# Two weight sums of a seven-product scheme moved into adding transfers, with six row tiles per block in place of five

## The chip, the cores and the metric

The kernel runs on one core of one Trainium2 chip. The metric is the device time of one execution in microseconds (us): the median of three runs, which lie between 1940.07 and 1940.61 us. One further execution was recorded by the profiler; its rows are what the text reads.

## The reference

One encoder layer over 256 tokens with a model width of 2048, all in float32. Each of its four sub-layers normalises its input, works, normalises again and adds to the residual `h`:

```
h += 1/2 * post(SwiGLU_1(pre(h)))          # FFN 1: gate and up 2048 -> 5632, down 5632 -> 2048
h += post(mixer(pre(h)) W_o)               # attention over 16 heads, W_qkv 2048 -> 6144
h += 1/2 * post(SwiGLU_2(pre(h)))          # FFN 2, as FFN 1
h += post(sigmoid(pre(h) W_g) * (p W_p))   # embedding

def _swiglu(u, w_gate, w_up, w_down):
    return (jax.nn.silu(u @ w_gate) * (u @ w_up)) @ w_down
```

The change concerns the two SwiGLU stages: the products `u @ w_gate` and `u @ w_up`.

## The kernel before

**Float32 from halves.** Each weight tile of 128 rows x 512 columns (256 KB) comes from memory into a raw buffer. `split` (L71) makes two tiles of it, `wh` by a cast on ScalarE (ACT, L77) and `wl = raw - wh` by a subtraction on VectorE (DVE, L78), two row tiles at a time wherever there are two. The activations exist as high and low halves too. `mac` (L92) then issues three matmuls per row tile: high by high, low by high, high by low (L104, L105, L106). There are six buffers of each half, each for two row tiles, so a split may run at most six buffers ahead of TensorE.

**Column blocks.** A SwiGLU stage walks over eleven blocks of 512 of the 5632 columns (L451). For each it makes gate and up for two token halves of 128, multiplies silu(gate) by up, turns the result with eight transposes on TensorE (`transposed_split`, L279, called later through `run_later`), and multiplies it by the matching 512 rows of `w_down` into four output blocks. These four `down` products (L438) are not issued at once: they wait in a list, and the next column block's code takes one out at each call of `fill()`, to give TensorE work while other engines prepare operands. One `down` is four row tiles by two token halves, 24 matmuls.

**The seven-product scheme.** Block 0 makes gate and up directly. Blocks 1 to 10 use `pair_product` (L164), which is therefore called ten times per stage, twenty times in all. It takes ten of the sixteen row tiles of the shared dimension and treats them as two groups of five (`ROWS`, L29; `RQ` is the group's size). Two token halves by two groups by two weights (gate `wa`, up `wb`) make a 2x2 by 2x2 block product, which the Strassen-Winograd scheme does with seven block products in place of eight. Four of the seven use the activations as they are (`a11`, `a12`, `a22`) or sums of them made once per stage (`s1` to `s4`, made by `token_sums`, L294); on the weight side four sums of blocks are needed in each call. The remaining six row tiles are multiplied the ordinary way, `rest` (L200), in a load of four tiles and one of two, for gate and for up.

In each call four raw blocks of five row tiles are loaded by `blocks` (L178): `ra1` and `ra2` from gate, `rb1` and `rb2` from up, each as one transfer of four row tiles (L181) and one of a single row tile (L183). The four weight sums are additions on DVE through `add` (L189; the loop's instruction is L193, an addition without a loop is L195):

- `ra1 += rb1`, then `ra1 += rb2`, then `rb2 = rb1 + rb2`, then `ra1 += ra2`.

The order of the products in the text, for all blocks but block 1, is: `a11`, `s1`, the transposes (`run_later`), `rest` of up, a `down`, `s2`, `s4`, a `down`, `s3`, `rest` of up, a `down`, `a12`, `a22`, a `down`, `rest` of gate twice. In block 1 (`rest_first`) both loads of `rest` of up come first. Results that are used twice are copied out of the accumulator by `kept` (L173, a copy on ACT at L175).

**Buffers and queues.** The raw blocks share four buffers (tag `raw_b`) of five row tiles. The other weight loads (L68) share three buffers of four row tiles. Four accumulators (tag `acc`) serve the products. Every transfer before the change is issued by SyncE (SP) on one queue. The build framework turns the program text into one fixed instruction list per engine and per queue, moving steps forward by its own estimates of time, and puts a wait wherever a buffer or an operand needs one; an engine runs its list strictly in order. GpSimd (POOL) does little: a few powers at the stage borders (L273).

**Stage border.** After block 10, four gain vectors for the output normalisation are loaded one by one (`gain`, L260, L506) into buffers that `kept` also uses (tag `part`, four of them), and the last `down` products run in two groups.

Of the kernel before, what the change touches and what calls it, by code (L numbers as in the profile page):

```python
# [8 lines left out]
F32 = mybir.dt.float32  # L9
F32R = mybir.dt.float32r  # L10
AF = mybir.ActivationFunctionType
ALU = mybir.AluOpType
# [3 lines left out]
P = 128  # L16
# [9 lines left out]
EPS = 1e-6  # L26
SUPER = 8
MID = 3
ROWS = (0, 1, 2, 3, 8), (4, 5, 6, 7, 9)  # L29
RQ = len(ROWS[0])  # L30
BIG = 3.0e38

# [2 lines left out]
def encoder_layer(ctx: ExitStack, tc: tile.TileContext, a: dict, out: bass.AP):  # L35
# [123 lines left out]
    def run_later():  # L159
        for job in later:  # L160
            job()
        later.clear()

    def pair_product(lhs, sums, wa, ca, wb, cb, fill, rest_first):  # L164

        rows1, rows2 = ([lhs[k] for k in ks] for ks in ROWS)
        a11, a12, a22 = of_tile(rows1, 0), of_tile(rows2, 0), of_tile(rows2, 1)
        s1, s2, s3, s4 = sums

        def bank(name):  # L170
            return ps_acc.tile([P, NB], F32, name=f"pair_{name}", tag="acc")

        def kept(name, x):  # L173
            t = ffn_pool[0].tile([P, NB], F32, name=name, tag="part", bufs=4)
            nc.scalar.copy(t, x)  # L175
            return t

        def blocks(w, j, c):  # L178
            raw = ffn_pool[0].tile([P, RQ, NB], F32, name="raw_b", bufs=4)
            rows_ = w[j * KB * P : (j + 1) * KB * P, c : c + NB]  # L180
            raw_loads.append(nc.sync.dma_start(raw[:, :KB], rows_.rearrange("(k p) n -> p k n", p=P)))  # L181
            k = ROWS[j][KB]
            nc.sync.dma_start(raw[:, KB], w[k * P : (k + 1) * P, c : c + NB])  # L183
            return raw

        def split_rows(raw):
            return sum((split(raw[:, k : min(k + 2, RQ)]) for k in range(0, RQ, 2)), [])

        def add(out_, x, y, op=ALU.add):  # L189
            n = x.shape[1] if len(x.shape) > 2 else 0  # L190
            for k in range(0, n, 2):
                j = slice(k, min(k + 2, n))
                nc.vector.tensor_tensor(out_[:, j], x[:, j], y[:, j], op=op)  # L193
            if not n:
                nc.vector.tensor_tensor(out_, x, y, op=op)  # L195

        nk = len(lhs)
        k_rest = [(k, min(KB, nk - k)) for k in range(2 * RQ, nk, KB)]

        def rest(w, k, n, c, accs_, last=False):  # L200
            parts = load_parts(w, k * P, n, c)
            for t, acc, lead in accs_:
                mac(acc, of_tile(lhs[k : k + n], t), parts, first=lead, last=last)

        def rest_b(i, last):
            rest(wb, *k_rest[i], cb, [(1, u1, i == 0), (0, u0, i == 0 and rest_first)], last=last)

        if rest_first:
            u0, u1 = bank("u0"), bank("u1")
            rest_b(0, False)  # L210
            run_later()
        ra1, rb1 = blocks(wa, 0, ca), blocks(wb, 0, cb)
        if rest_first:
            rest_b(1, False)
        rb2 = blocks(wb, 1, cb)
        g1, s_ = bank("g1"), bank("g0" if rest_first else "u0")
        mac(g1, a11, split_rows(ra1), first=True, last=True)
        g0_ = kept("g0_s", g1)
        add(ra1, ra1, rb1)
        mac(s_, s1, split_rows(ra1), first=True, last=True)  # L220
        u1_ = kept("u1_s", s_)
        run_later()
        add(ra1, ra1, rb2)
        if rest_first:
            g0 = s_
        else:
            u0, u1 = s_, bank("u1")
            rest_b(0, False)
        fill()
        mac(g1, s2, split_rows(ra1), last=True)  # L230
        u0_ = kept("u0_s", g1)
        if rest_first:
            add(u0_, u0_, u1_, ALU.subtract)
        mac(u0, s4, split_rows(rb2), last=rest_first)
        add(rb2, rb1, rb2)
        ra2 = blocks(wa, 1, ca)
        fill()
        mac(g1, s3, split_rows(rb2), last=True)
        if not rest_first:
            rest_b(1, True)  # L240
        add(u0_, u0, u0_, ALU.subtract)
        add(u1_, u1_, g1, ALU.subtract)
        add(u1_, u1, u1_)
        fill()
        if not rest_first:
            g0 = bank("g0")
        mac(g0, a12, split_rows(ra2), first=True)
        add(ra1, ra1, ra2)
        mac(g1, a22, split_rows(ra1))
        fill()  # L250
        for k, n in k_rest:
            rest(wa, k, n, ca, [(0, g0, False), (1, g1, False)], last=k + n == nk)
        assert len(k_rest) == 2
        add(g0_, g0, g0_)
        return (g0_, g1), (u0_, u1_)
# [87 lines left out]
    def load_x(k):  # L343
        if k % 2:
            return
        hi, lo = (u[:, k % KB : k % KB + 2] for u in x_blocks[k // KB])
        if k < 2 * RQ:
            if k == 0:
                x_kept.append(ffn_pool[0].tile([P, RQ, 2, S], F32, name="xb", tag="raw_b", bufs=4))
            xb = x_kept[0][:, k // 2]  # L350
        else:
            xb = ffn_pool[0].tile([P, 2, S], F32, name="xb", tag="gs", bufs=2)
        nc.sync.dma_start(xb, xT[:, k : k + 2])
        for i in range(2):
            g = row_g[:, 0, k + i : k + i + 1]
            nc.scalar.activation(hi[:, i], xb[:, i], AF.Copy, scale=g)
            nc.vector.scalar_tensor_tensor(
                lo[:, i], xb[:, i], g, hi[:, i].bitcast(F32), op0=ALU.mult, op1=ALU.subtract
            )
        if k < 2 * RQ:  # L360
            x_first.append(xb)
# [16 lines left out]
    def residual(fg, ssf, scale, blocks, rs, g, sums=None, y_pool=None):  # L378

        blocks += [new_split(acts, "u", D // NB) for _ in range(D // NB)]
        r, y0 = [], []
        for b0 in range(0, D // NB, 2):
            for t in range(NT):
                if b0 == 0:
                    r.append(rsqrt_mean(ssf[t], D, scale))
                for b in range(b0, b0 + 2):
                    cols = slice(b * NB, (b + 1) * NB)
                    fg_t = last_f.pop(t) if b == D // NB - 1 and t in last_f else fg[:, t, cols]  # L390
                    nc.vector.scalar_tensor_tensor(
                        h[:, t, cols], fg_t, r[t], h[:, t, cols], op0=ALU.mult, op1=ALU.add
                    )
                    y = transposed_split(
                        h[:, t, cols], *blocks[b], t, g[:, b * KB : (b + 1) * KB],
                        **(dict(pool=y_pool, tag="y0", bufs=6) if b < 3 and y_pool is not None else {}),
                    )
                    if b < 3:
                        y0.append(y)
                yield  # L400
        if sums is not None:
            later.append(
                lambda: sums.extend(
                    token_sums(
                        *([y[:, i : i + 2] for y in y0[:4]] for i in (0, 2)),
                        [y[:, i : i + 1] for y in y0[4:] for i in (0, 1)],
                    )
                )
            )
        later.append(lambda: rs.extend(prenorm_factor(t) for t in range(NT)))  # L410
# [4 lines left out]
    def swiglu(pool, f, ssf, res, blocks, rs, sums, w_gate, w_up, w_down, g_post):  # L415
# [35 lines left out]
        for nb in range(nbs):  # L451
            c0 = nb * NB
            if True:
# [3 lines left out]
                else:  # L457
                    gate, up = accs("gate"), accs("up")
                    if rs is None:
# [6 lines left out]
                        def ahead_up(k):  # L466
                            load_h(k)
                            if k == KB:
                                with tc.issue_after(splits[0].ins), tc.issue_after(splits[1].ins):
                                    for i, x in enumerate(x_first):  # L470
# [2 lines left out]
                                    half = [slice(t * P, (t + 1) * P) for t in range(NT)]  # L473
                                    sums[:] = token_sums(
                                        *([x[:, :, h_] for h_ in half for x in x_first[i:4:2]] for i in (0, 1)),
                                        [x_first[4][:, i : i + 1, h_] for h_ in half for i in (0, 1)],
                                    )

                        product(gate, lhs, w_gate, 0, c0, steps=steps, ahead=ahead_gate)
# [6 lines left out]
                if nb < nbs - 1:  # L486
                    hid = new_split(pool, "hid", 1)
                else:
                    both = pool.tile([P, 2, KB, S], F32R, name="hid_2", tag="raw_b", bufs=4)
                    hid = both[:, 0], both[:, 1]  # L490
                for t in range(NT):
                    y = up[t] if nb > 0 else pool.tile([P, NB], F32, name="hm", tag="part", bufs=4)
                    nc.vector.scalar_tensor_tensor(y, up[t], rs[t], gs[t], op0=ALU.mult, op1=ALU.mult)
                    later.append(lambda y=y, s_=hid, t=t: transposed_split(y, *s_, t))
            if nb < nbs - 1:
# [4 lines left out]
            job()  # L500
        run_later()
        hrows = rows([hid])
        for cols in ((0,), (1, 2, 3)):
            blocks_ = []
            for b in cols:
                gp = gain(pool, g_post, b * NB, "g_post", "part", 4)  # L506
                ps, tag = (ps_acc, "acc") if b in (1, 2) else (ps_o, "o")
                acc = [ps.tile([P, NB], F32, name=f"down{t}", tag=tag) for t in range(NT)]
                blocks_.append((b, gp, acc, load_parts(w_down, nb * NB, KB, b * NB)))
# [342 lines left out]
```

## Time and profile before

| what | value |
| --- | --- |
| median of three runs | 1940.18 us |
| the profiled execution's own time | 1942.38 us |
| its span (first to last recorded instruction) | 1940.6 us |
| mean granted TensorE clock | 0.998 of full speed |
| TensorE instructions (matmuls and transposes) | 8660 |
| DVE busy | 1597.2 us |
| ACT busy | 1096.2 us |
| POOL busy | 25.4 us |
| moved by transfers | 376.95 MB |

How to read it: PE is TensorE's matmuls, PEld its weight loads, DVE is VectorE, ACT is ScalarE, POOL is GpSimd, SPq is SyncE's transfer queue. A row of the grouped view gives line, engine, operation, the names of output and inputs, their shapes and the count, then busy us and the mean ns of one, then the idle time of the engine just before them with what ended it. A row of the timeline gives start, duration, engine, line, operation and names. A row of the view by stretches gives, for each engine, busy us and in brackets its instructions, then the granted clock, the busy share of the sixteen DMA engines and GB/s. A matmul's recorded duration overlaps the next one's; how fast TensorE works is read from the distance of their starts.

### The profile page before, as it was taken

How to read it: one execution, taken by the hardware profiler on the slowest of the kernel's cores; microseconds unless marked ns; L12 is line 12 of the kernel's file. 1: busy time of each engine (PE TensorE's matmuls, PEld its weight loads, DVE VectorE, ACT ScalarE, POOL GpSimd, SP SyncE). 2: the span in 40 equal slices, each digit the busy share in tenths (PEclk: the TensorE clock that was granted, in tenths of full speed). 3: DMA queues.
4: the chain of work that ended last, by engine and by line, in shares of the span. 5: the costliest groups of instructions: out<-in, count | busy, mean ns of one | idle time of the engine just before them, and what ended most of it. 6: DMA issues, size and time to landing. Idle time of an engine off the chain costs nothing.

```text
span 1940.6 us, 23428 instructions
## 1 busy us (share of the span) xinstructions
PE 1915.1 (99%) x8660; PEld 1574.0 (81%) x8660; DVE 1597.2 (82%) x1881; ACT 1096.2 (56%) x1404; POOL 25.4 (1%) x31
## 2 busy tenths in 40 slices
PE   8999999999999999999999999999999999999998
PEld 6888888888888878888888888888888888888786
DVE  7898899989998976656565589998999899988864
ACT  7565555556555554554545466655655555555653
POOL 0000000000000000000000000000000000000000
PEclk9999999999999999999999999999999999999999
DMA  9646644665446446454455566456544664464463
GB/s 353 222 168 223 250 168 172 213 228 198 180 176 217 167 144 243 151 190 145 159 174 176 193 213 227 174 200 227 201 180 173 228 231 172 154 220 175 139 233 114
DMA packets 191586, 376.95 MB, mean 194 GB/s; under 512 B 7664, under 2 KB 10736, under 8 KB 191216
## 3 DMA queue, kind: packets, MB, share of 16 engines
q1 hardware_dynamic: 191472, 375.46, 54.8%
q8 instruction: 68, 1.11, 0.2%
q14 instruction: 46, 0.38, 0.1%
HBM read 373.33 MB, written 2.10 MB: 193 GB/s over the span
## 4 chain that ended last, share of the span: by engine, by line
PE 95%; DVE 3%; issue 1%; ACT 1%; DMA 1%; POOL 0%; SPq 0%; DVEq 0%; POOLq 0%; ACTq 0%
PE pair_g L105 9%; PE pair_g L104 9%; PE pair_g L106 9%; PE down L105 8%; PE down L106 8%; PE down L104 8%; PE pair_u L105 5%; PE pair_u L104 5%; PE pair_u L106 5%; PE v L106 1%; PE v L104 1%; PE mo L104 1%; PE v L105 1%; PE mo L106 1%; PE mo L105 1%; PE tr L284 1%
## 5 line engine op out<-in xcount | busy, mean ns | idle before, releaser
L78 DVE TENSOR_TENSOR wl<-raw,wh 128x1024 fp32r<-128x1024 f32 (+1 forms) x493 | 588.8, 1220 | 157.2 <-ACT wh L77 145.4
L77 ACT CAST wh<-raw 128x1024 fp32r<-128x1024 f32 (+1 forms) x493 | 510.0, 1050 | 311.5 <-PE pair_g L105 43.9
L77 ACT CAST wh<-raw_b 128x1024 fp32r<-128x1024 f32 (+1 forms) x420 | 376.7, 907 | 389.4 <-PE down L105 167.1
L78 DVE TENSOR_TENSOR wl<-raw_b,wh 128x1024 fp32r<-128x1024 f32 (+1 forms) x420 | 428.7, 1044 | 64.1 <-ACT wh L77 64.0
L105 PE MATMUL down<-wh,hid_l 128*128 128x512 f32 x640 | 252.3, 394 | 0.0
L104 PE MATMUL down<-wh,hid_h 128*128 128x512 f32 x640 | 251.2, 393 | 0.0
L106 PE MATMUL down<-wl,hid_h 128*128 128x512 f32 x640 | 249.2, 390 | 0.4 <-DVE wl L78 0.4
L193 DVE TENSOR_TENSOR raw_b<-raw_b 128x1024 f32<-128x1024 f32 (+1 forms) x240 | 245.0, 1045 | 1.2
L106 PE MATMUL pair_g<-wl,u_h 128*128 128x512 f32 x540 | 210.1, 389 | 0.0
L105 PE MATMUL pair_g<-wh,u_l 128*128 128x512 f32 x540 | 210.1, 389 | 0.0
L104 PE MATMUL pair_g<-wh,u_h 128*128 128x512 f32 x540 | 210.1, 389 | 0.0
L104 PEld LDWEIGHTS down<-wh,hid_h 128*128 128x128 f32 x640 | 120.2, 188 | 27.8
L106 PEld LDWEIGHTS down<-wl,hid_h 128*128 128x128 f32 x640 | 120.2, 188 | 27.8 <-DVE wl L78 0.8
L105 PEld LDWEIGHTS down<-wh,hid_l 128*128 128x128 f32 x640 | 120.4, 188 | 24.5
L430 DVE TENSOR_TENSOR f<-f,down 128x512 f32<-128x512 f32 x160 | 109.4, 683 | 16.0 <-PE down L106 15.7
L104 PEld LDWEIGHTS pair_g<-wh,u_h 128*128 128x128 f32 x540 | 101.4, 188 | 21.2
L106 PEld LDWEIGHTS pair_g<-wl,u_h 128*128 128x128 f32 x540 | 101.4, 188 | 21.1
L105 PEld LDWEIGHTS pair_g<-wh,u_l 128*128 128x128 f32 x540 | 101.3, 188 | 21.1
L104 PE MATMUL pair_u<-wh,u_h 128*128 128x512 f32 x240 | 95.2, 397 | 0.0
L106 PE MATMUL pair_u<-wl,u_h 128*128 128x512 f32 x240 | 93.5, 390 | 0.0
L105 PE MATMUL pair_u<-wh,u_l 128*128 128x512 f32 x240 | 93.5, 389 | 0.0
L105 PE MATMUL pair_g<-wh,sums_l 128*128 128x512 f32 x210 | 82.8, 394 | 0.0
(218 smaller groups left out, 2989.9 us busy)
## 6 DMA issues: line engine op xcount, KB each, us to landing
raw<-in_ffn_w_down SPq DMA_DIRECT2D x88, 1024.0 KB, 6.2
raw<-in_w_qkv SPq DMA_DIRECT2D x48, 1024.0 KB, 5.0
raw_b<-in_ffn_w_gate SPq DMA_DIRECT2D x40, 1024.0 KB, 5.1
raw_b<-in_ffn_w_up SPq DMA_DIRECT2D x40, 1024.0 KB, 7.1
raw<-in_ffn_w_up SPq DMA_DIRECT2D x28, 1024.0 KB, 5.1
raw<-in_ffn_w_gate SPq DMA_DIRECT2D x27, 1024.0 KB, 5.1
raw<-in_w_o SPq DMA_DIRECT2D x16, 1024.0 KB, 5.0
raw<-in_w_ple_gate SPq DMA_DIRECT2D x16, 1024.0 KB, 5.0
```

The source lines that it names most:

```text
L77: nc.scalar.copy(wh[:, :n], raw),
L78: nc.vector.tensor_tensor(wl[:, :n], raw, wh[:, :n].bitcast(F32), op=ALU.subtract),
L104: nc.tensor.matmul(acc, xh, wh, start=lead, stop=False, skip_group_check=True)
L105: nc.tensor.matmul(acc, xl, wh, start=False, stop=False, skip_group_check=True)
L106: nc.tensor.matmul(acc, xh, wl, start=False, stop=tail, skip_group_check=True)
L193: nc.vector.tensor_tensor(out_[:, j], x[:, j], y[:, j], op=op)
L284: nc.tensor.transpose(tr[:, k], x[:, k * P : (k + 1) * P], ident)
L430: nc.vector.tensor_tensor(f_t, f_t, acc, op=ALU.add)
```

## The change

- `ROWS` becomes two groups of six row tiles: twelve row tiles take the seven products, four are left for `rest`, which loads them two and two.
- `rb1` is no longer loaded. Two of the four sums are made by transfers: `add_rows` reads the up block's first group from memory again and adds it into a buffer that already holds something. It is issued by GpSimd on its own queue with `accum_op=ALU.add`, in three transfers of two row tiles (512 KB) each. It is called for `ra1` after the product `a11` has used it, and for `rb2` after `ra1 += rb2` has used it. `ra1 += rb2` and `ra1 += ra2` stay on DVE.
- A raw block is loaded as one transfer of four and one of two row tiles; `raw_b` has three buffers of six row tiles.
- New order: `a11`, `s4`, the transposes, `s1`, `rest` of up, a `down`, `s2`, a `down`, `s3`, `rest` of up, a `down`, `a12`, `a22`, a `down`, `rest` of gate twice. In block 1 a `down` stands between `s4` and `s1`. `s1` has an accumulator of its own, so `u0_ - u1_` is now subtracted in every call.
- `part` has three buffers; the four gain vectors are loaded by one transfer into a `raw_b` buffer. The token sums cover six row tiles. The scratch for software-made descriptors grows from 512 to 2048.

```
-ROWS = (0, 1, 2, 3, 8), (4, 5, 6, 7, 9)
+ROWS = (0, 1, 2, 3, 8, 9), (4, 5, 6, 7, 10, 11)
...
+        def add_rows(raw, w, j, c):
+            for k0, k1 in spans(j, 2):
+                nc.gpsimd.dma_start(raw[:, k0:k1], weight_rows(w, j, c, k0, k1), accum_op=ALU.add)
...
-        k_rest = [(k, min(KB, nk - k)) for k in range(2 * RQ, nk, KB)]
+        k_rest = [(k, (nk - 2 * RQ) // 2) for k in range(2 * RQ, nk, (nk - 2 * RQ) // 2)]
...
-        ra1, rb1 = blocks(wa, 0, ca), blocks(wb, 0, cb)
+        ra1, rb2 = blocks(wa, 0, ca), blocks(wb, 1, cb)
         if rest_first:
             rest_b(1, False)
-        rb2 = blocks(wb, 1, cb)
-        g1, s_ = bank("g1"), bank("g0" if rest_first else "u0")
+        g1 = bank("g1")
         mac(g1, a11, split_rows(ra1), first=True, last=True)
         g0_ = kept("g0_s", g1)
-        add(ra1, ra1, rb1)
-        mac(s_, s1, split_rows(ra1), first=True, last=True)
-        u1_ = kept("u1_s", s_)
+        add_rows(ra1, wb, 0, cb)
+        u0 = u0 or bank("u0")
+        mac(u0, s4, split_rows(rb2), first=not rest_first, last=rest_first)
         run_later()
+        if rest_first:
+            fill()
+        g0 = bank("g0")
+        mac(g0, s1, split_rows(ra1), first=True, last=True)
+        u1_ = kept("u1_s", g0)
         add(ra1, ra1, rb2)
-        if rest_first:
-            g0 = s_
-        else:
-            u0, u1 = s_, bank("u1")
+        add_rows(rb2, wb, 0, cb)
+        if not rest_first:
+            u1 = bank("u1")
             rest_b(0, False)
         fill()
         mac(g1, s2, split_rows(ra1), last=True)
         u0_ = kept("u0_s", g1)
-        if rest_first:
-            add(u0_, u0_, u1_, ALU.subtract)
-        mac(u0, s4, split_rows(rb2), last=rest_first)
-        add(rb2, rb1, rb2)
+        add(u0_, u0_, u1_, ALU.subtract)
         ra2 = blocks(wa, 1, ca)
         fill()
         mac(g1, s3, split_rows(rb2), last=True)
...
-                gp = gain(pool, g_post, b * NB, "g_post", "part", 4)
+                gp = gains[:, b]
...
-dynamic_dma_scratch_size=512
+dynamic_dma_scratch_size=2048
```

More of the change, by code (lines that the diff above doesn't have):

```diff
@@ L173, in kept, with spans, weight_rows @@
         def kept(name, x):
-            t = ffn_pool[0].tile([P, NB], F32, name=name, tag="part", bufs=4)
+            t = ffn_pool[0].tile([P, NB], F32, name=name, tag="part", bufs=3)
             nc.scalar.copy(t, x)
             return t
-        def blocks(w, j, c):
[L179 to L183, printed above, removed]
-            return raw
+        def spans(j, step):
+            for k0, k1 in ((0, KB), (KB, RQ)):
+                for k in range(k0, k1, step):
+                    yield k, min(k + step, k1)
+        def weight_rows(w, j, c, k0, k1):
+            r0 = ROWS[j][k0] * P
+            return w[r0 : r0 + (k1 - k0) * P, c : c + NB].rearrange("(k p) n -> p k n", p=P)
+        def blocks(w, j, c):
+            raw = ffn_pool[0].tile([P, RQ, NB], F32, name="raw_b", bufs=3)
+            for k0, k1 in spans(j, KB):
+                raw_loads.append(nc.sync.dma_start(raw[:, k0:k1], weight_rows(w, j, c, k0, k1)))
+            return raw
+        def add_rows(raw, w, j, c):
+            for k0, k1 in spans(j, 2):
+                nc.gpsimd.dma_start(raw[:, k0:k1], weight_rows(w, j, c, k0, k1), accum_op=ALU.add)
         def split_rows(raw):
@@ L206, in rest_b @@
             rest(wb, *k_rest[i], cb, [(1, u1, i == 0), (0, u0, i == 0 and rest_first)], last=last)
+        u0 = u1 = None
         if rest_first:
@@ L243, in pair_product @@
         add(u1_, u1, u1_)
-        fill()
         if not rest_first:
-            g0 = bank("g0")
+            fill()
         mac(g0, a12, split_rows(ra2), first=True)
@@ L348, in load_x @@
             if k == 0:
-                x_kept.append(ffn_pool[0].tile([P, RQ, 2, S], F32, name="xb", tag="raw_b", bufs=4))
+                x_kept.append(ffn_pool[0].tile([P, RQ, 2, S], F32, name="xb", tag="raw_b", bufs=3))
             xb = x_kept[0][:, k // 2]
@@ L405, in residual @@
                         *([y[:, i : i + 2] for y in y0[:4]] for i in (0, 2)),
-                        [y[:, i : i + 1] for y in y0[4:] for i in (0, 1)],
+                        [y[:, i : i + 2] for y in y0[4:] for i in (0, 2)],
                     )
@@ L475, in ahead_up @@
                                         *([x[:, :, h_] for h_ in half for x in x_first[i:4:2]] for i in (0, 1)),
-                                        [x_first[4][:, i : i + 1, h_] for h_ in half for i in (0, 1)],
+                                        [x_first[i][:, :, h_] for h_ in half for i in (4, 5)],
                                     )
@@ L488, in swiglu @@
                 else:
-                    both = pool.tile([P, 2, KB, S], F32R, name="hid_2", tag="raw_b", bufs=4)
+                    both = pool.tile([P, 2, KB, S], F32R, name="hid_2", tag="raw_b", bufs=3)
                     hid = both[:, 0], both[:, 1]
                 for t in range(NT):
-                    y = up[t] if nb > 0 else pool.tile([P, NB], F32, name="hm", tag="part", bufs=4)
+                    y = up[t] if nb > 0 else pool.tile([P, NB], F32, name="hm", tag="part", bufs=3)
                     nc.vector.scalar_tensor_tensor(y, up[t], rs[t], gs[t], op0=ALU.mult, op1=ALU.mult)
@@ L502, in swiglu @@
         hrows = rows([hid])
+        gains = pool.tile([P, D // NB, NB], F32, name="gains", tag="raw_b", bufs=3)
+        nc.sync.dma_start(gains, bass.AP(tensor=g_post.tensor, offset=g_post.offset, ap=[[0, P], [NB, D // NB], [1, NB]]))
         for cols in ((0,), (1, 2, 3)):
@@ L840 @@
     arrays = {k: np.ascontiguousarray(v) for k, v in arrays.items()}
-    nc = bacc.Bacc("TRN2", target_bir_lowering=False, num_devices=1, dynamic_dma_scratch_size=512)
+    nc = bacc.Bacc("TRN2", target_bir_lowering=False, num_devices=1, dynamic_dma_scratch_size=2048)
     aps = {
```

## The prediction

> **What bounds the kernel now.** I read the page first, then the stretches of one column block each, the waits, the groups by form and the timelines.
>
> ```profile
> span 1940.6 us, 23428 instructions
> PE 1915.1 (99%) x8660; PEld 1574.0 (81%) x8660; DVE 1597.2 (82%) x1881; ACT 1096.2 (56%) x1404; POOL 25.4 (1%) x31
> 312.10:375.23 63.13, 63.13 (x283) 52.09 (x282) 58.01 (x64) 36.43 (x43) 0.00 (x0) 1.00 0.57 200
> 375.23:438.36 63.13, 63.13 (x282) 52.10 (x282) 58.01 (x64) 36.43 (x43) 0.00 (x0) 1.00 0.56 200
> PE gate L104 <- ACT wh L77: 7.5, 2, 5.8
> PE down L106 <- DVE wl L78: 0.4, 1, 0.4
> ACT wh L77 <- PE down L105: 206.0, 118, 3.1
> ACT wh L77 <- PE pair_g L105: 148.6, 183, 3.5
> ```
>
> The third and fourth lines are two successive column blocks: 63.13 us each, PE busy throughout (third number), DVE 58.01, ACT 36.43, POOL nothing, clock 1.00, DMA engines 0.57 and 0.56 busy. PE's own longest wait is at the start of the kernel (gate). ACT, on the contrary, waits for PE in hundreds of splits: the operands run ahead until the six `wh` buffers are full. So TensorE's instruction stream is the time. A column block gets faster only by fewer matmuls, and slower only if something makes PE wait.
>
> **The matmuls.** The groups by form give counts, the timeline their distance.
>
> ```profile
> L104 PE MATMUL pair_g<-wh,u_h 128*128 128x512 f32 x540 | 210.1, 389 | 0.0
> L104 PE MATMUL pair_u<-wh,u_h 128*128 128x512 f32 x240 | 95.2, 397 | 0.0
> L104 PE MATMUL pair_g<-wh,sums_h 128*128 128x512 f32 x210 | 82.7, 394 | 0.0
> L104 PE MATMUL pair_u<-wh,sums_h 128*128 128x512 f32 x190 | 74.8, 394 | 0.0
> 339.57 0.39 PE L104 MATMUL pair_g<-wh,sums_h 128*128 128x512 f32 x1
> 343.00 0.39 PE L104 MATMUL pair_u<-wh,u_h 128*128 128x512 f32 x1
> 351.21 0.39 PE L104 MATMUL pair_g<-wh,u_h 128*128 128x512 f32 x1
> 358.01 0.39 PE L104 MATMUL down<-wh,hid_h 128*128 128x512 f32 x1
> 363.51 0.39 PE L104 MATMUL pair_g<-wh,u_h 128*128 128x512 f32 x1
> 371.67 0.39 PE L104 MATMUL pair_g<-wh,u_h 128*128 128x512 f32 x1
> 378.51 1.04 PE L284 MATMUL tr<-ident,u_s 128*128 128x128 f32 x8
> 379.30 0.48 PE L104 MATMUL pair_u<-wh,u_h 128*128 128x512 f32 x1
> ```
>
> Of the L104 form, 540 + 240 = 780 use `u` and 210 + 190 = 400 use `sums`; over twenty calls and three forms that is 117 and 60 per call, as the code says: three products of five tiles x 3 and six rest tiles x 12, then four products x 15. After: 3 x 18 + 4 x 12 = 102 and 4 x 18 = 72. So 174 for 177: 300 fewer with `u`, 240 more with `sums`, net 60 fewer. The distances: `s3` is 15 matmuls from 339.57 to 343.00, 0.2287 us each; `a12` and `a22` are 30 from 351.21 to 358.01, 0.2267 each; a `down` is 24 from 358.01 to 363.51, 0.2292. The change: 300 x 0.2267 = 68.0 off, 240 x 0.2287 = 54.9 on, **13.1 us off**, all on the path. Bounds: 60 x 0.2267 = 13.6 if the larger sums tile ran as `u` does, 300 x 0.2267 - 240 x 0.2292 = 13.0 as `down` does.
>
> **DVE, ACT.** They are not on the path, and stay off it.
>
> ```profile
> L78 DVE TENSOR_TENSOR wl<-raw_b,wh 128x1024 fp32r<-128x1024 f32 x280 | 338.4, 1223 | 64.1 <-ACT wh L77 64.0
> L193 DVE TENSOR_TENSOR raw_b<-raw_b 128x1024 f32<-128x1024 f32 x160 | 195.0, 1222 | 1.2
> L78 DVE TENSOR_TENSOR wl<-raw_b,wh 128x512 fp32r<-128x512 f32 x140 | 96.3, 688 | 0.0
> L77 ACT CAST wh<-raw_b 128x512 fp32r<-128x512 f32 x140 | 86.9, 621 | 92.8 <-PE pair_u L105 39.4 <-PE pair_g L105 30.6 <-PE down L105 9.4
> L193 DVE TENSOR_TENSOR raw_b<-raw_b 128x512 f32<-128x512 f32 x80 | 55.1, 689 | 0.0
> L195 DVE TENSOR_TENSOR u_s<-u_s,pair_g 128x512 f32<-128x512 f32 x20 | 13.7, 686 | 0.3 <-PE pair_g L106 0.2
> ```
>
> Per call the sums were 4 x (2 x 1.222 + 0.689) = 12.5 us and become 2 x 3 x 1.222 = 7.3; the subtraction now done in every call adds 0.69; the low halves were 7 x (2 x 1.223 + 0.688) + 6 x 1.223 = 29.3 and become (21 + 4) x 1.223 = 30.6. DVE loses 3.2 us of 58.01. ACT's casts go from 7 x (2 x 1.05 + 0.621) + 6 x 1.05 = 25.3 to 25 x 1.05 = 26.3 us, 1.0 more beside 26.7 us of idleness. Both count nothing. If the DVE relief freed a PE wait, it could give no more than the 0.4 us above, so I take nothing.
>
> **The adding transfers: how long they may take.** This is the new wait. TensorE waits for a sum if its last 512 KB piece lands late. The issue time follows from the buffers: a split starts when PE lets go of the `wh` tile six splits earlier.
>
> ```profile
> 358.27 1.04 ACT L77 CAST wh<-raw_b 128x1024 fp32r<-128x1024 f32 x1
> 362.11 1.05 ACT L77 CAST wh<-raw_b 128x1024 fp32r<-128x1024 f32 x1 [2.80 <-PE down L105]
> 363.48 0.62 ACT L77 CAST wh<-raw_b 128x512 fp32r<-128x512 f32 x1 [0.33 <-DMA raw<-in_ffn_w_down]
> 364.93 0.68 DVE L78 TENSOR_TENSOR wl<-raw_b,wh 128x512 fp32r<-128x512 f32 x1
> ```
>
> These are `a11`'s three splits; PE starts `a11` at 371.67 (36 rest matmuls after 363.51). The first waits for the end of `a22` (358.01), the second for three quarters of the `down` (358.01 + 4.1), the third for its end, and 2.1 us after the third cast starts its low half is done.
>
> After the change, with PE's start of `a11` at 0: before it lie two rest units of 12 matmuls (-5.4), the `down` (-10.9), `a22` (-15.0). `a11`'s splits start at the second third of `a22` (-12.3), its end (-10.9), and three quarters of the `down` (-6.8). With 2.2 us for cast and subtraction, the pieces for `ra1` can be issued at -10, -8.7 and -4.6. PE then does `a11` (18, 4.1 us), `s4` (4.1) and the transposes (378.51 to 379.30, 0.8): `s1` starts at 9.0. Its third split is used 12 matmuls later, at 11.7, and must have begun 2.2 us before, less the 0.45 until the low half is wanted: 9.9. So the pieces have 17, 17 and **14 us**. The pieces for `rb2` wait for `ra1 += rb2`, done by about 8; `s3` starts at 31, its first split must begin at 29, so they have 20 us, and 15 in block 10, where one `down` is left out here. In block 1 the `down` put ahead of `s1` adds 5.5 us.
>
> ```profile
> q1 hardware_dynamic: 191472, 375.46, 54.8%
> DMA to landing us min/median/max: 3.9/5.7/13.8
> raw_b<-in_ffn_w_up SPq DMA_DIRECT2D x40, 1024.0 KB, 7.1
> raw<-in_ffn_w_up SPq DMA_DIRECT2D x20, 512.0 KB, 3.5
> ```
>
> No transfer of before adds, and none comes from POOL. The nearest rows: a plain 512 KB lands in 3.5 us (lower bound; less is excluded, as the bytes are the same and one more operand is read); the slowest `raw_b` load of the run took 13.8 (second line, upper bound). I take 7, twice 3.5, because each word is read twice. All three are under 14: the sum stays unchanged. The Trainium skill, DMA: Bandwidth & Descriptors, Anatomy of one DMA, fits 2.0 us + bytes / 436 GB/s for a transfer written by GpSimd, an estimate of 3.2 us for 512 KB without adding; by it the sum is also 13.1 us off.
>
> Engine time: 0.548 x 1940.6 x 16 / 191472 = 89 ns per packet (a row of 2 KB). Plain row tiles per column block fall from 48 (20 + 12 + 16) to 42, adding ones are 12: six row tiles more are read, 1.6 MB. Plain: 42 x 128 x 89 / 16 = 29.9 us of 62.5; adding at the same price 8.5, at twice 17.1, together 47, or 75%. The engines are full at 340 ns per adding packet, 3.8 times a plain one.
>
> POOL's queue has nothing behind the waiting issues in a column block (0.00 busy above). Fewer, larger `raw_b` buffers: three blocks share three, as four shared four.
>
> ```profile
> 331.29 0.37 SPq L181 DMA_DIRECT2D raw_b<-in_ffn_w_gate  x1
> ```
>
> Before, this load of `ra1` went out 27 us ahead of its first split (358.27). After, `ra1` can take the buffer that `rb2` leaves once `s3` is split, at about 27, and its first split is at 62.5 - 12.3 = 50: 23 us for loads of 7.1. SP's queue is relieved of the `rb1` loads. I cost both at nothing; if that cover were gone, a late `ra1` would eat into the 14 us above first.
>
> **Borders.** The token sums grow by one row tile per group. Once per stage four additions go from the second form below to the first, 0.13 each, two subtractions of low halves grow by about twice that, and in the first stage one multiply of 128x512 is added (0.69 by the rows above): 1.8 us of DVE at most.
>
> ```profile
> L308 DVE TENSOR_TENSOR y_s<-xb,y_s 128x256 f32<-128x256 f32 x2 | 0.8, 424 | 0.0
> L308 DVE TENSOR_TENSOR y_s<-xb,y_s 128x128 f32<-128x128 f32 x1 | 0.3, 290 | 0.0
> 1160.00:1170.00 10.00, 10.00 (x46) 8.29 (x45) 7.36 (x8) 4.26 (x5) 0.00 (x0) 1.00 1.05 401
> 687.33 1.05 ACT L77 CAST wh<-raw 128x1024 fp32r<-128x1024 f32 x1 [0.33 <-PE down L105]
> 679.47 0.37 SPq L68 DMA_DIRECT2D raw<-in_ffn_w_down  x1
> ```
>
> PE is busy without a gap just behind the second stage's sums (1160 to 1170, DVE 7.36 of 10): nothing, at most 1.8 twice. The gains' 1 MB in one load may hold up the last `down` load by 768 KB, 2 us at the 401 GB/s of the full engines; issued at 679.47, it is used at 687.33, after a wait for PE, so nothing, at most 2 twice.
>
> **Sum.** Against the profiled execution's own 1942.38: 1942.38 - 13.1 = 1929.3. The median of before lies 2.2 below that execution: 1940.18 - 13.1 = **1927.1 us**. Its own range is 1926 (13.6 off) to 1934 (borders at their bounds, 7.6 together).
>
> **Rivals.**
> First, slower: the third piece for `ra1` lands too late. It decides from 14 us; each us beyond costs about 18 (twenty calls without the two of block 1). At 14.7 the gain is gone, at 16 the time is 1927 + 2 x 18 = 1963. For it: an adding packet of over 340 ns fills the DMA engines and any lateness then accumulates; writing the descriptors is software, with no row here. Against: 14 us is twice my value. Chance 0.10.
> Second, slower: the fixed order puts `s1`'s splits behind the copies of the turned result. The `tr` rows end at 9.0; two copies (about 1.1 us) and a cast (1.05) follow before `s1`, some 2.1 us per call, 1927 + 38 = 1965. Against: rest's splits, due in the same place, were started ahead of those copies in the timeline of before. Chance 0.05.
> Third, slower: descriptors get written only while DVE is idle. DVE has 63.13 - 58.01 = 5.1 us of idleness in a block, and in the stretch where `rb2`'s pieces are issued there is hardly any, so they could be 7 us late at `s3`: 1927 + 140 = 2067. Chance 0.03. The Trainium skill, SBUF — State Buffer, "SBUF: two separate sides", tells of such a starving, but for DVE's two-port modes, which it denies to `tensor_tensor`; the DVE rows above (1222 ns for 1024 elements per partition) fit that, so the rule speaks against the change only in name.
> Fourth, no change: about 0.65 us per call is lost somewhere along these waits (a third piece at 14.7 us, or the plain loads of `w_down` pushed late by the extra traffic), and eats 13 us: 1940. Chance 0.10.
>
> **The numbers.** Forecast 0.72, rivals 0.10, 0.05, 0.03, 0.10. A measurement tells 0.2% (3.9 us) from no change: faster is below 1936.3, slower above 1944.1. So faster 0.72, same 0.10, slower 0.18. The range starts at 1926, a little below the bound of the matmuls left out, and reaches through the fourth case to 1944; the slower ones, 0.18, lie above.
>
> **What would show it.** Right: a column block of 62.4 to 62.5 us with PE busy throughout; L104 to L106 counts of 680 with `u` and 480 with `sums`; DVE near 55 us per block; the pieces landing in 4 to 10 us; no wait of `s1`'s or `s3`'s splits for a transfer that reaches PE. Wrong: PE gaps ahead of `pair_g` or `pair_u` with `sums`, released by a cast that waits for POOL's transfer; PE distances other than 0.227 to 0.229; a DMA share above 0.9.

## The result and the profile after

The changed kernel takes 1963.07 us (median of four runs, 1957.0 to 1963.99), beside 1940.12 us of the kernel before on the same chip: a ratio of 1.0111 over the single runs (the medians alone give 1.0118), interval 1.0091 to 1.0132. It is slower by 1.1%. The forecast of 1927.1 us missed by 36 us, and the time lies above the range.

The first lines of the page of after: the span, the engines, and SP's queue (q1) and POOL's (q0), each with packets, MB and share of sixteen engines' span.

```profile
span 1962.2 us, 23327 instructions
PE 1914.2 (98%) x8600; PEld 1565.5 (80%) x8600; DVE 1552.7 (79%) x1740; ACT 1119.0 (57%) x1364; POOL 173.0 (9%) x151
q1 hardware_dynamic: 174608, 344.00, 51.1%
q0 software_dynamic: 32640, 62.92, 18.2%
```

TensorE has 60 instructions fewer, as worked out. Yet it is now idle 48 us of the span (1962.2 - 1914.2), against 25.5 before (1940.6 - 1915.1). The matmuls went; waiting came in their place. Two successive column blocks, from one block's transposes to the next's:

```profile
318.51:382.85 64.34, 62.84 (x279) 51.45 (x278) 55.67 (x56) 37.66 (x42) 7.33 (x6) 1.00 0.78 221
382.85:447.05 64.20, 62.78 (x279) 51.45 (x278) 55.88 (x57) 37.84 (x42) 7.34 (x6) 1.00 0.78 221
```

A block takes 64.3 us where 63.13 was the time before and 62.4 to 62.5 the forecast; 1.4 to 1.5 us in it are TensorE idle. DVE is busy 55.7 us, so no engine is the bound in its place. The view of waits names the idle time (us in total, times, longest):

```profile
PE pair_u L106 <- DVE wl L78: 25.1, 18, 2.9
...
ACT wh L77 <- DMA raw_b<-in_ffn_w_up: 60.4, 40, 3.6
```

Eighteen waits: one in each of the twenty calls but the two of block 1. (Sixteen are in the first `rest` of up; in the two blocks 10 it is the second `rest` that waits, 0.6 and 0.3 us.) TensorE waits in `pair_u` for a low half. The only transfers that ACT's splits of the raw blocks wait for are POOL's adding ones. The chain of waits joins the two (start, duration, what):

```profile
365.04 1.21 POOL raw_b L195
...
370.52 11.20 DMA raw_b<-in_ffn_w_up
381.81 1.06 ACT wh L77
382.89 1.23 DVE wl L78
384.12 3.12 DVE raw_b L204 x3
...
387.44 0.73 DVE hid_l L302 x2
...
388.64 1.22 DVE wl L78
389.91 0.50 PE pair_u L106
```

Read it from the end. At 389.91 TensorE gets the low half of the first weights of `rest` of up. DVE made it at 388.64, after the low halves of the turned result, after the three additions of `ra1 += rb2`, after the low half of `s1`'s third split. That split waited for the third adding piece, which POOL issued at 370.52 and which landed 11.2 us later. And the matmuls at that place, from the timeline (start, duration, in brackets the idle time before):

```profile
386.49 0.39 PE L104 MATMUL pair_g<-wh,sums_h 128*128 128x512 f32 x1
...
388.10 0.39 PE L105 MATMUL pair_u<-wh,u_l 128*128 128x512 f32 x1
389.91 0.50 PE L106 MATMUL pair_u<-wl,u_h 128*128 128x512 f32 x1 [1.42 <-DVE wl L78]
390.24 0.39 PE L104 MATMUL pair_u<-wh,u_h 128*128 128x512 f32 x1
```

The row at 386.49 is the first matmul of `s1` that uses the third piece. It starts without a wait: `s1` itself is in time. Its low half was done at 384.12 and is wanted two matmuls later than 386.49, at 386.9, some 2.8 us afterwards. The wait is in the next product, `rest`, whose weights have nothing to do with the adding transfer and had been in the core for long.

**The books.** The same instruction lists without the adding (e3 below) have a span of 1925.7, so 36.5 us are to be explained. Listed waits: 25.1. Around each wait the starts are stretched besides: from 388.10 to 390.24 there are 2.14 us where two matmuls at 0.23 take 0.46, so 1.68 are lost for a listed 1.42; 0.26 x 18 = 4.7. After three of the waits TensorE's clock was lowered for some microseconds, about 6 us in all (last section). The sum is 36 us. The single runs fit the last term: three of the four took 1962.75 to 1963.99 us at a mean granted clock of 0.994 to 0.995, the fourth 1957.0 us at 0.998.

**The adding transfers.** POOL's transfers into the raw blocks: duration of the issue on POOL (ns, minimum, median, maximum), and the time from issue to landing (us).

```profile
L195 POOL DMA_DIRECT2D raw_b<-in_ffn_w_up x120: 1203/1219/1442, 56.3 to 1769.7; - x120
...
DMA to landing us min/median/max: 5.7/10.2/13.7
```

The median is 10.2 us; I had taken 7. While the first set is under way the engines are full (last three numbers: granted clock, DMA share, GB/s; a share above 1 means that the recorded times of packets overlap):

```profile
363.00:366.00 3.00, 3.00 (x15) 2.44 (x13) 2.72 (x3) 1.42 (x2) 0.96 (x1) 1.00 0.93 350
372.00:375.00 3.00, 3.00 (x15) 2.49 (x14) 1.83 (x2) 1.33 (x2) 0.00 (x0) 1.00 1.12 237
378.00:381.00 3.00, 3.00 (x14) 2.45 (x14) 2.40 (x3) 1.05 (x1) 0.00 (x0) 1.00 0.54 102
```

Plain loads of the next weights fill them, and POOL's pieces, issued from 365.04 on, share them; from 372 to 375 they are still full, at a lower rate, and only from 378 on is there room. The Trainium skill, DMA: Bandwidth & Descriptors, "Issuing engines are not separate DMA queues", says that transfers from all issuers run on the same sixteen engines and interleave. The trace agrees (shares of 0.93 and 1.12 with both at work): POOL's queue of its own saves SP's time, not the engines'.

### The profile page after: what moved, and what is told of

Read it like the earlier page. It is cut to its first block, busy times and chain, and to the rows that moved or that the text cites. A ratio compares the mean times of both kernels' runs of the same rounds, so it can differ in the third digit from the quotient of the medians.

```text
span 1962.2 us, 23327 instructions
## 1 busy us (share of the span) xinstructions
PE 1914.2 (98%) x8600; PEld 1565.5 (80%) x8600; DVE 1552.7 (79%) x1740; ACT 1119.0 (57%) x1364; POOL 173.0 (9%) x151
## 3 DMA queue, kind: packets, MB, share of 16 engines
q0 software_dynamic: 32640, 62.92, 18.2%
## 4 chain that ended last, share of the span: by engine, by line
PE 76%; DMA 8%; DVE 8%; issue 4%; ACT 2%; POOL 2%; POOLq 0%; DVEq 0%; ACTq 0%; SPq 0%
DMA raw_b<-in_ffn_w_up 8%; PE pair_g L105 7%; PE pair_g L104 7%; PE down L105 7%; PE pair_g L106 7%; PE down L104 7%; PE down L106 7%; DVE wl L78 3%; PE pair_u L106 3%; DVE raw_b L204 2%; PE pair_u L105 2%; PE pair_u L104 2%; ACT wh L77 2%; POOL raw_b L195 2%; PE v L106 1%
## 5 line engine op out<-in xcount | busy, mean ns | idle before, releaser
L77 ACT CAST wh<-raw 128x1024 fp32r<-128x1024 f32 (+1 forms) x453 | 469.1, 1051 | 374.2 <-PE down L105 104.6
L78 DVE TENSOR_TENSOR wl<-raw,wh 128x1024 fp32r<-128x1024 f32 (+1 forms) x453 | 543.9, 1218 | 140.2 <-ACT wh L77 126.8
L77 ACT CAST wh<-raw_b 128x1024 fp32r<-128x1024 f32 x420 | 436.5, 1050 | 334.6 <-PE down L105 130.5
L78 DVE TENSOR_TENSOR wl<-raw_b,wh 128x1024 fp32r<-128x1024 f32 x420 | 505.0, 1220 | 145.5 <-ACT wh L77 138.9
L195 POOL DMA_DIRECT2D raw_b<-in_ffn_w_up x120 | 146.8, 1267 | 1081.5 <-DVE wl L78 772.9
L106 PE MATMUL pair_g<-wl,u_h 128*128 128x512 f32 x520 | 202.3, 389 | 0.0
L104 PE MATMUL pair_g<-wh,sums_h 128*128 128x512 f32 x360 | 143.1, 397 | 0.0
L204 DVE TENSOR_TENSOR raw_b<-raw_b 128x1024 f32<-128x1024 f32 x120 | 142.7, 1217 | 0.1
L105 PE MATMUL pair_g<-wh,sums_l 128*128 128x512 f32 x360 | 141.7, 394 | 0.0
L106 PE MATMUL pair_g<-wl,sums_h 128*128 128x512 f32 x360 | 141.3, 393 | 0.0
## 6 DMA issues: line engine op xcount, KB each, us to landing
raw_b<-in_ffn_w_up POOLq DMA_DIRECT2D x120, 512.0 KB, 10.2
```

The source lines that it names most:

```text
L77: nc.scalar.copy(wh[:, :n], raw),
L78: nc.vector.tensor_tensor(wl[:, :n], raw, wh[:, :n].bitcast(F32), op=ALU.subtract),
L104: nc.tensor.matmul(acc, xh, wh, start=lead, stop=False, skip_group_check=True)
L105: nc.tensor.matmul(acc, xl, wh, start=False, stop=False, skip_group_check=True)
L106: nc.tensor.matmul(acc, xh, wl, start=False, stop=tail, skip_group_check=True)
L195: nc.gpsimd.dma_start(raw[:, k0:k1], weight_rows(w, j, c, k0, k1), accum_op=ALU.add)
```

## Experiments

My theory after this reading: the adding transfers land too late for what is queued behind the split that waits for them, and DVE's and ACT's fixed order passes the lateness on to `rest`. Rivals: the adding transfers slow everything by their traffic alone, whatever the order; the second set (into `rb2`) matters as much; or the matmul term was wrong and the waits only show it.

**e1: the additions behind `rest`.** Only the place of `ra1 += rb2` and of the second set is changed, so that the low half of `rest` is made directly behind `s1`'s.

```
         u1_ = kept("u1_s", g0)
-        add(ra1, ra1, rb2)
-        add_rows(rb2, wb, 0, cb)
         if not rest_first:
             u1 = bank("u1")
             rest_b(0, False)
+        add(ra1, ra1, rb2)
+        add_rows(rb2, wb, 0, cb)
```

> The sum ra1 += rb2 on VectorE and the second set of adding transfers stand behind the first rest load of up in the text; only VectorE's list changes (rest's low half now directly behind the splits of s1). Theory A (the third adding piece lands about 11 us after its issue, in time for s1 itself, but VectorE's list puts three additions and the turned result's low halves ahead of rest's low half, and TensorE waits for that): the wait of 1.2 to 2.9 us per column block falls below 0.4 us, the clock stays at 1.00, 1927 to 1935 us. Theory B (the traffic of the adding transfers itself is the cost, whatever the order): no less than 1955 us. Theory C (the pieces are too late for s1 itself): TensorE waits in front of s1, 1950 us or more.

Measured: 1943.71 us (before 1940.08), ratio 1.0017, 1.0008 to 1.0026: 19.4 us better than the change, not the 1927 to 1935 that I had hoped for. Its waits:

```profile
PE pair_u L104 <- ACT wh L77: 3.3, 2, 2.0
PE down L106 <- DVE wl L78: 2.9, 4, 1.0
```

The eighteen waits are gone, so the three additions did stand in front of `rest`'s low half. What is left has moved on. DVE's timeline just behind the late piece of one block (start, duration):

```profile
378.04 1.23 DVE L78 TENSOR_TENSOR wl<-raw_b,wh 128x1024 fp32r<-128x1024 f32 x1 [1.29 <-ACT wh L77]
379.47 1.23 DVE L78 TENSOR_TENSOR wl<-raw,wh 128x1024 fp32r<-128x1024 f32 x1 [0.20 <-ACT wh L77]
380.61 2.35 DVE L204 TENSOR_TENSOR raw_b<-raw_b 128x1024 f32<-128x1024 f32 x2
382.88 1.28 DVE L302 TENSOR_TENSOR hid_l<-tr,hid_h 128x512 fp32r<-128x512 f32 x2
384.08 1.21 DVE L204 TENSOR_TENSOR raw_b<-raw_b 128x1024 f32<-128x1024 f32 x1
```

DVE stands idle for 1.29 us before the third split's low half, and from then on it works with one gap of 0.20; the next consumers, a `down` in some blocks and the second `rest` in both blocks 10, get their operands late. TensorE's waits there, 0.4 to 2.0 us each, sum to 7.6 of the 15.7 us that e1 lies above e3 (below); the rest was not followed up.

**e2: `rest` ahead of `s1`.** The splits of `rest` no longer stand behind the split that waits.

```
         if rest_first:
             fill()
+        else:
+            u1 = bank("u1")
+            rest_b(0, False)
         g0 = bank("g0")
         mac(g0, s1, split_rows(ra1), first=True, last=True)
...
-        if not rest_first:
-            u1 = bank("u1")
-            rest_b(0, False)
```

> The first rest load of up and its 12 matmuls stand ahead of the product s1 in the calls other than block 1, so s1 is wanted 2.7 us later and rest's split is ahead of s1's on ScalarE and VectorE. Theory A: no wait per column block above 0.3 us, 1926 to 1933 us, no worse than the kernel with only the sum moved. Theory B (traffic): 1955 us or more. Theory C (late for s1 itself): better than the changed kernel by about 2.7 us per call at the most, so near 1927 as well, but with waits in front of s1 where the list alone is changed.

Measured: 1931.08 us, ratio 0.9955, 0.9941 to 0.9969. One block of it, and its landing time:

```profile
311.62:374.09 62.47, 62.47 (x280) 51.52 (x278) 55.04 (x57) 37.31 (x41) 7.29 (x6) 1.00 0.81 227
```

```profile
DMA to landing us min/median/max: 5.7/10.1/13.9
```

TensorE is busy throughout in 62.47 us, the forecast's block, with the transfers as slow as before and the engines as full (0.81). So the rival of the traffic alone falls: it is traffic and order together. What stays is in the two blocks 10, where one `down` is left out ahead of `s3`: the third piece for `rb2` is issued at 629.17 and its split begins at 640.18, and the second `rest` of up stands behind that split, as the first one did behind `s1`'s. TensorE waits there for 0.74 and 0.72 us in the first stage (642.23 and 643.68). In the first stage the profile names a matmul as what released that split; in the second it names the transfer (2.37 us, the split at 1748.28), and TensorE waits 0.71 us behind it.

**e3: the same lists, plain transfers.** POOL issues the same 120 transfers without the addition; every engine's list is the same.

```
-                nc.gpsimd.dma_start(raw[:, k0:k1], weight_rows(w, j, c, k0, k1), accum_op=ALU.add)
+                nc.gpsimd.dma_start(raw[:, k0:k1], weight_rows(w, j, c, k0, k1))
```

> The same transfers, from the same queue at the same places, but they copy instead of adding (the two sums are not made, the output is not the reference's); every engine's list is the same. Theory A: a packet costs the transfer engines about 92 ns in place of 175, the third piece lands in 6 to 8 us in place of 11.2, so the splits of s1 no longer wait for it, and the wait behind VectorE's list falls to 0 to 0.6 us per column block: 1927 to 1940 us. Theory D (VectorE's list alone makes the wait, also with pieces in time): 1.2 us per block stay, 1955 us or more. If issuing by GpSimd rather than the adding makes the latency: landing still above 9 us and about 1960 us.

Measured: 1928.06 us, ratio 0.9942, 0.9928 to 0.9956. Its page's line on POOL's queue, and the same rows of L195 as above:

```profile
q0 software_dynamic: 17280, 62.92, 9.1%
```

```profile
L195 POOL DMA_DIRECT2D raw_b<-in_ffn_w_up x120: 724/724/872, 56.5 to 1733.0; - x120
...
  ACT wh L77: 0.2, 1
...
DMA to landing us min/median/max: 4.0/5.6/9.3
```

The same bytes, from the same engine in the same order, cost half the engine time (9.1% for 18.2%) and land in 5.6 us for 10.2. I had expected cheaper packets, 92 ns for 175; the page shows half as many instead (17280 for 32640), at 162 ns each. The size of a packet is not the reason: SP's plain queue moves about 2 KB a packet, as the adding one does, and costs as little per byte as the plain transfers here (last section). A single split waited for one of them, 0.2 us. So all of the loss of 35.0 us (1963.07 - 1928.06) hangs on the addition in the transfer, given the change's order; and the order removes nearly all of it, given the addition (e2).

**e4: the first set left out.**

```
         g0_ = kept("g0_s", g1)
-        add_rows(ra1, wb, 0, cb)
```

> The adding transfers into ra1 are left out (s1 and what follows use an incomplete sum, the output is not the reference's); the second set stays, the lists keep their order. Theory A: nothing is waited for at s1's splits, no TensorE wait of more than 0.3 us per column block, 62.4 to 62.5 us per block, 1926 to 1931 us: the pure gain of 60 matmuls. Theory D (the list alone): 1 us per block stays, 1950 us. If the second set matters too: waits in front of s3.

Measured: 1929.0 us, ratio 0.9943, 0.9929 to 0.9957. The second set alone lands in

```profile
DMA to landing us min/median/max: 5.8/7.8/12.2
```

and TensorE waits once behind it, 0.7 us in one block 10. The rival of the second set falls: its 20 us are enough. The first set, with 14 us to its own consumer, made the loss.

**e5: `rest` ahead, and a `down` ahead of `s3` in block 10 too.** In block 10 the list of `down` products has two empty places, the second and the fourth; the second is the one ahead of `s3`. They become the third and the fourth.

```
-                    waiting[1:1], waiting[3:3] = [None], [None]
+                    waiting[2:2] = [None, None]
```

> As the kernel with rest ahead of s1, and in block 10 the two calls of fill that do nothing are the third and fourth in place of the second and fourth, so a down stands between s2 and s3 there too. Theory A (the second set of pieces is late only in block 10, where that down is missing; TensorE waits 0.7 us twice there and the block is 1.1 to 1.9 us longer in each stage): both blocks lose this, 1927 to 1929.5 us. If the block's extra time has another cause: 1931 as before.

Measured: 1928.87 us (1927.31 to 1929.02; before 1939.99), ratio 0.9941, 0.9928 to 0.9953. It is faster than both kernels. A block of it:

```profile
310.26:372.73 62.47, 62.47 (x279) 51.53 (x278) 55.59 (x56) 37.77 (x42) 7.29 (x6) 1.00 0.81 228
```

**e6: e2 with groups of five row tiles.** The adding transfers and the new order without the larger groups; `ROWS` and the two places of the token sums go back to five.

```
-ROWS = (0, 1, 2, 3, 8, 9), (4, 5, 6, 7, 10, 11)
+ROWS = (0, 1, 2, 3, 8), (4, 5, 6, 7, 9)
```

> As the kernel with rest ahead of s1, but with groups of five row tiles as before the change (rest loads three and three): the adding transfers and the new order without the sixth row tile. If the gain is the 60 matmuls alone: 13 us above it, 1942 to 1945 us, a column block at 63.1 us in the first stage. If moving sums off VectorE or the order gives something by itself: 1938 us or less.

Measured: 1939.64 us, ratio 0.9998, 0.9989 to 1.0008: no difference from the kernel before. I had expected 1942 to 1945, 13 us above e2; it lies 8.6 above e2 and 10.8 above e5. Its block is the old one:

```profile
311.72:374.84 63.12, 63.12 (x282) 52.09 (x281) 53.97 (x61) 37.06 (x45) 6.68 (x6) 1.00 0.78 222
```

So with five row tiles the adding transfers and the order are worth nothing: they take DVE from 58.0 to 54.0 us a block, and DVE was not the bound.

**e7: six row tiles, e2's order, no adding transfers.** SP loads `rb1` into the third large buffer, and all four sums are on DVE.

```
-        ra1, rb2 = blocks(wa, 0, ca), blocks(wb, 1, cb)
+        ra1, rb1, rb2 = blocks(wa, 0, ca), blocks(wb, 0, cb), blocks(wb, 1, cb)
...
-        add_rows(ra1, wb, 0, cb)
+        add(ra1, ra1, rb1)
...
-        add_rows(rb2, wb, 0, cb)
+        add(rb2, rb2, rb1)
```

> As the kernel with rest ahead of s1, but no adding transfer: the up block's first group is loaded by SyncE into the third buffer and both sums are made on VectorE, six additions more per call (7.3 us, VectorE busy about 62 us by the sum of its rows in a block of 62.5). If the adding transfers are needed to keep VectorE off the path: waits of TensorE for low halves, 1935 us or more. If VectorE still has room (its instructions overlap by about 7%): 1926 to 1930 us, at least as good as with adding transfers. If the three buffers are too few for four blocks: waits for raw_b loads, 1940 us or more.

Measured: 1936.34 us, ratio 0.9982, 0.9973 to 0.9991. Block 1 and a later block:

```profile
55.93:129.05 73.12, 69.10 (x303) 55.83 (x302) 70.75 (x67) 51.97 (x60) 0.00 (x0) 1.00 0.52 179
317.00:379.67 62.67, 62.67 (x279) 51.46 (x278) 61.76 (x63) 37.82 (x41) 0.00 (x0) 1.00 0.58 202
```

In the later block DVE is busy 61.76 of 62.67 us, and TensorE is still busy throughout. A steady block is hardly slower than e2's in the first stage (62.67 for 62.47) and no slower in the second (62.87 for 62.95). The loss is in block 1: there DVE does 70.75 us, and the block takes 73.12 where e2's and e5's take 67.95 from the same transposes to the next (71.09 for 68.56 in the second stage). TensorE waits there for low halves from DVE (0.53, 0.64 and 1.19 us), and for 1.67 us (at 58.64) for a cast of `rest` that ACT, in this build's list, does only after casting the turned result; how much of the loss is DVE's and how much this order's is not separated. No split waits for a load into `raw_b`. So the transfers that add show a worth in block 1 alone. In program order e7's nearest partner is e2, and e7 is 5.3 us slower (1936.34 - 1931.08); against e5, which has block 10 mended besides, 7.5. The kernels differ in the raw buffers' loads too, so the difference is theirs together.

## Why the prediction was wrong

**The step that failed** is the one headed "The adding transfers: how long they may take". It asked by when TensorE's start of `s1` wants the third piece, found 14 us, and let everything below it pass: "All three are under 14: the sum stays unchanged." The 14 us were right: the piece took 11.2 and `s1` had 2.8 to spare, together 14.0. But a split that waits for a transfer holds ACT's and DVE's lists, and I did not name what is queued behind it. Behind it stood `ra1 += rb2` (3.1 us), the turned result's low halves and the low half of `rest`, which TensorE wants right after `s1`. TensorE was ready for that low half at 388.33 (388.10 plus one matmul) and began with it at 389.91, 1.58 late, so the piece could have taken some 9.6 us, an estimate from this one block: 4.4 less than I allowed. The other blocks agree. From the third issue to the start of its split it took 10.8, 11.3 and 12.9 us in the blocks with waits of 0.78, 1.42 and 2.93 us (TensorE at 1644.43, 581.98 and 1252.50), one us of wait for each of lateness; in the first stage's block 10 it took 9.8, and the first `rest` there waited no more than 0.1 us (644.38 to 644.71). My sign of being wrong, gaps ahead of products with `sums`, did not come for the same reason: the gaps stand ahead of a product with `u`. The first rival had this mechanism's price, some 18 us for each us of lateness, and the wrong point from which it decides.

**The landing time** was the term that was mis-sized: 7 us, taken as twice the plain 3.5, where 10.2 is the median. The bound of 13.8 held in the changed kernel (13.7 at most; 13.9 in e2). The 3.5 was the median of a load at another place of the block; POOL's plain pieces in the change's place take 5.6 (e3), and twice that would have been 11.2, more than the 9.6.

**The engine's price** was right: "twice" gave a DMA share of 75% per block, and 0.78 was measured. An average over a block of 62 us says nothing of the 15 us in which the plain loads and the adding ones meet.

**The matmuls** were right. The counts are as worked out:

```profile
L104 PE MATMUL pair_g<-wh,u_h 128*128 128x512 f32 x520 | 202.3, 389 | 0.0
L104 PE MATMUL pair_g<-wh,sums_h 128*128 128x512 f32 x360 | 143.1, 397 | 0.0
L104 PE MATMUL pair_u<-wh,u_h 128*128 128x512 f32 x160 | 64.6, 404 | 0.0
L104 PE MATMUL pair_u<-wh,sums_h 128*128 128x512 f32 x120 | 47.2, 394 | 0.0
```

520 + 160 = 680 with `u`, 360 + 120 = 480 with `sums`. Where nothing waits for POOL, a block takes 62.47 (e2, e5) or 62.49 us (e3), and the time is 1928.06 (e3) or 1928.87 (e5): 12.0 and 11.1 below before, where 13.1 was forecast. The difference of e5 and e6 gives 10.8 for the same term, with other border work in it. Per block the forecast was 0.65 us; it is 0.66 in the first stage (63.13 to 62.47) and 0.59 in the second (63.53 to 62.94, e5). Where the rest of the missing 1 to 2 us went was not traced.

**DVE** was right in size and wrong in use. The additions fell from 250.1 us (195.0 + 55.1) to 142.7 (the 120 of L204), 5.4 us a call where 5.2 was worked out; a block's busy time fell by 2.3 us (58.01 to 55.7) where 3.2 was (in e2 by 3.0). "Both count nothing" holds for a block's total, and it hid that DVE's order in a 10 us stretch does count. That the relief of DVE brings nothing holds for five row tiles (e6); with six, block 1 is longer without it (e7).

**The other rivals.** The second did not come: the cast of the turned result stands behind `s1`'s splits, not ahead. Nor did the third: POOL's issues took 1203 to 1442 ns, and the three for `rb2`, where I feared it, took 3.71 us together from 385.90 on, though DVE is busy all of the 4 us from 386 to 390. The Trainium skill's rule in SBUF — State Buffer, "SBUF: two separate sides", had no effect here; its exception for `tensor_tensor` agrees with that. The buffers, the borders and the gains' load cost nothing that shows: from the first stage's last transposes to the second stage's first it takes 483.2 us before and 480.7 in e5. Block 10, where I gave `rb2`'s pieces 15 us, repeats the failed step: `s3` was in time, and the `rest` behind its splits was not (e2).

**Shown and not shown.** That the loss needs both the addition in the transfer and the order is shown (e2, e3). How much of the 10.2 us is the adding itself and how much the meeting with plain loads is not separated; the fastest pieces give a bound, 5.7 us adding and 4.0 plain.

## What to carry to other kernels

A new wait on an in-order engine is costed by everything queued behind it, not only by the operand that it waits for: list what stands behind the waiting instruction on each engine, when TensorE wants each, and take the smallest slack. Work that doesn't need the late operand belongs ahead of the wait; here moving one load's splits made a loss of 23 us a gain of 9, and with block 10 mended, of 11. A transfer's time is taken from the stretch in which it will run, not from the median of another.

## What the runs showed of the hardware

**Adding in a transfer costs twice the engine time.** 62.92 MB on POOL's queue took 18.2% of sixteen engines' 1962.2 us when adding, 0.182 x 1962.2 x 16 / 62.92 = 90.8 us of one engine per MB, and 44.6 when plain (0.091 x 1925.7 x 16 / 62.92); SP's plain queue in after took 46.6. An issue takes POOL 1219 ns when adding, 724 when plain.

**Short waits can lower TensorE's clock.** After a wait of 2.13 us the matmuls first ran at 0.23 us apart, then at 0.425, then at 0.23 again; after one of 2.23 us they did not slow down (timeline of after):

```profile
131.17 0.50 PE L106 MATMUL pair_u<-wl,u_h 128*128 128x512 f32 x1 [2.13 <-DVE wl L78]
...
132.22 0.63 PE L104 MATMUL pair_u<-wh,u_h 128*128 128x512 f32 x1
132.64 0.63 PE L105 MATMUL pair_u<-wh,u_l 128*128 128x512 f32 x1
...
135.62 0.39 PE L106 MATMUL down<-wl,hid_h 128*128 128x512 f32 x1
...
1320.64 0.50 PE L106 MATMUL pair_u<-wl,u_h 128*128 128x512 f32 x1 [2.23 <-DVE wl L78]
1320.98 0.40 PE L104 MATMUL pair_u<-wh,u_h 128*128 128x512 f32 x1
1321.21 0.40 PE L105 MATMUL pair_u<-wh,u_l 128*128 128x512 f32 x1
```

The slow stretch lasts from 132.22 to 135.62, 3.4 us, eight matmuls at 0.195 more: 1.6 us lost. Of the other two, one lasts 3.3 us (from 1514.83) and one 5.5 (from 1253.09). The granted clock agrees (the number ahead of the DMA share):

```profile
130.00:135.00 5.00, 3.83 (x11) 3.06 (x12) 5.00 (x5) 2.11 (x4) 0.86 (x1) 0.72 1.08 192
1321.00:1326.00 5.00, 5.00 (x23) 4.11 (x22) 5.00 (x5) 1.28 (x2) 0.00 (x0) 1.00 1.11 220
```

Of the eighteen waits those of 2.00, 2.13 and 2.93 us were followed by such a stretch, those of 1.92 and 2.23 and all shorter ones were not. A wait of 2.2 us at the start of the attention stage, which every run has, shows the same: a slow stretch follows it in e3 (705.19) and e5 (704.19), none in after (721.90) and e2 (707.55). The Trainium skill, TensorE: Matmul & The Clock Gate, Part 1, tells of a monitor with a free-running window of about 3.4 us that halves the clock after an idle window. The halving agrees with the rows, and so do 3.4 us for two of the three stretches. A free-running window could be why 2.13 us sufficed once and 2.23 didn't, but no wait here is as long as 3.4 us, so a window that must be idle throughout does not explain the rows. The Trainium skill's advice on the same page, "Why this matters for your kernels", to avoid idle gaps above some 3 us is too lax here: 2.0 us was enough once. What decides was not tried; it cost 6 of the 36 us.
